# Both gates of a two-layer encoder from seven quarter products: the first gate changed over, and the last weight casts of a gate requeued

## The chip, the cores and the metric

The kernel runs on one core of one Trainium2 chip. The metric is the device time of one execution in microseconds; the time before is the median of three runs. Engines are named as in the profile: PE multiplies matrices (PEld is its weight load), DVE, ACT and POOL work on vectors, SP and others issue transfers.

## The reference

Two layers over 512 tokens of width 1024. Each layer is a mixer (neighbourhood attention, then latent attention) with a SiLU gate and a residual, followed by a gated embedding:

```
for i in range(DEPTH):
    xn = rmsnorm(x, norm_g[i])
    y = mixer_na(...) if i % 2 == 0 else mixer_mla(...)
    h = x + y
    gate = jax.nn.sigmoid(rmsnorm(h, ple_norm[i]) @ ple_w_gate[i])
    x = h + gate * (p[i] @ ple_w_proj[i])
return rmsnorm(x, final_norm)
```

The line with `gate` is what the change is about: a product of 512x1024 by 1024x1024 in each layer.

## The kernel before, in words

All products are made of float32 values split into a high part (`hi`, a rounded copy) and the rest (`lo`): one product of two split operands is three products on PE (hi by hi, lo by hi, hi by lo). So a weight of 128x1024 values costs a load into `wraw`, a copy on ACT (`whi`, L83 or L588) and a subtraction on POOL, sometimes on DVE (`wlo`, L84 or L590), before PE can use it.

The order in time: the embedding products of layer 0 and the first projections; neighbourhood attention in eight pairs of heads (`na_heads`, loop over `j`, each step projecting pair j+1 and attending pair j); the output projection of layer 0 (`out_proj`), the first gate, the latent projection of layer 1 (`mla_c`), latent attention (`mla_heads`), the output projection and gate of layer 1, and the last norm. A framework places the instructions of each engine in a fixed order when the program is built, by a simulated timeline; `issue_after(x)` says that an instruction may not be placed ahead of x. Each engine runs its queue in order.

There are two ways to make a gate. `gate_phase` (used in layer 0 before) takes each of four row tiles of 128 tokens by each of two column halves: 24 products of 512 columns for each of these eight pieces, 192 in all. `gate_seven` (used in layer 1) cuts rows, inner dimension and columns in two and makes the result from seven products of quarters in place of eight, each a quarter of rows in two blocks `i` of 128 tokens by 512 columns: 7 x 2 x 12 = 168 products. It needs sums and differences of the operand's quarters (`keep_half`, `operand`, `mixed`, into tiles X1 to X7) and four sums of the weight's quarters. These are made in DRAM: `sums_begin` issues four copies of 1 MB each on SP's queue, `sums_add` four accumulating transfers on POOL's queue (L528), in three steps, during the first pairs of `na_heads`.

`gate_seven` runs the products in the order 1, 7, 2, 6, 5, 3, 4. `prep(p)` loads, casts and subtracts the two weight pieces of product p. Products 1, 7 and 6 begin a bank of PSUM for each block; 2 adds into 1's, 5 and 3 into 6's, 4 into 7's. Between them ACT copies a bank (`s1`, `s17`, `s6`, the last at L651) and DVE subtracts. `finish(t, n, ...)` makes of a finished bank the sigmoid, multiplies the embedding product to it, adds it to the residual row tile `t`, half `n`, and puts the follow-up (`after`) on a list `behind` that the next `finish` empties. Blocks of product 2 finish half 0 of tiles 0 and 1, of 5 half 1 of tiles 2 and 3, of 3 half 1 of tiles 0 and 1, of 4 half 0 of tiles 2 and 3.

The follow-up in layer 0 is `done`: when both halves of a row tile are there, the tile goes to DRAM (`spill`), its norm is taken (square on ACT, mean on DVE, power on POOL, scaling on DVE), eight transposes on PE turn it and ACT and DVE split it into `x1T`, the operand of `mla_c`. `mla_c` makes first 384 columns for the four row tiles, 24 products each, then 288.

PSUM banks are taken by name: "mm" has 2, "S" 2, "T" 3, "O" 1; transposes use "T".

Of the kernel before, what the change touches and what calls it, by code (L numbers as in the profile page):

```python
# [25 lines left out]
EPS = 1e-6  # L26
# [2 lines left out]
NWARM = 11  # L29
NLATE = 3  # L30
NEARLY = 7
SEVEN = (1,)


def win(t, r0, r1, off, dims):
# [5 lines left out]
class Trunk:  # L41
# [182 lines left out]
    def na_heads(self, pool, xT, zs, oT):  # L224
        nc, a = self.nc, self.a
# [87 lines left out]
        last = project(0)  # L313
        for j in range(8):
            if j < 7:
                last = project(j + 1)
            attend(j)
            for l in SEVEN:
                if j == 0:
                    with self.tc.issue_after(self.last_bias.ins):  # L320
                        self.sums_begin(l)
                elif j < 4:
                    with self.tc.issue_after(self.last_norm.ins):
                        self.sums_add(l, j - 1)
        late = range(8 - NLATE, 8)
        zs.update(self.z_phase(a["na_z"], xT, late, self.last_exp.ins))
        for j in late:
# [242 lines left out]
    def gate_seven(self, pool, layer, rh, res, after):  # L570

        nc = self.nc
        pieces = 0
        turns = 3 + self.wxn // 2
        W, A, Bk, s1, s17, s6 = {}, {}, {}, {}, {}, {}

        def prep(p):
            nonlocal pieces
            W[p] = []
            src = self.quarter[layer][p] if p < 4 else self.sums[layer][p]  # L580
            for c in range(2):
                own = pieces % turns < 3
                pieces += 1
                raw = self.wp.tile([P, 1024], F32, name="wraw", tag="wraw", bufs=3)
                q, n = (self.wp, 3) if own else (pool, self.wxn)
                hi, lo = (q.tile([P, 1024], F32R, name=t, tag=t if own else "w4", bufs=n) for t in ("whi", "wlo"))
                nc.sync.dma_start(raw, src[c * P:(c + 1) * P])
                nc.scalar.activation(hi, raw, AF.Copy)  # L588
                for o in (slice(0, S), slice(S, 2 * S)):
                    nc.gpsimd.tensor_tensor(out=lo[:, o], in0=raw[:, o], in1=hi[:, o].bitcast(F32), op=ALU.subtract)  # L590
                W[p].append((hi, lo))

        behind, loaded = [], self.last_load

        def finish(t, n, ps, o=0, wd=S, last=False):
            x = ps
            sg = nc.scalar.activation(x, x, AF.Sigmoid, scale=rh[t])
# [7 lines left out]
            nc.vector.tensor_tensor(out=x, in0=pe, in1=ps, op=ALU.mult)  # L605
            r = res[t][:, n * S + o:n * S + o + wd]
            (nc.vector if last else nc.gpsimd).tensor_tensor(out=r, in0=r, in1=x, op=ALU.add)
            behind.append(lambda: after(t, n, o, wd))

        mm = self.last_out  # L610
        order = (1, 7, 2, 6, 5, 3, 4)
# [2 lines left out]
        warm = self.small.tile([P, 1], F32, name="warm", tag="ss")  # L614
        nc.scalar.activation(warm, rh[3], AF.Sigmoid)
        halves = ((0, 256), (256, 256)) if layer == 1 else ((0, S),)
        banks = {1: "mm", 7: "T", 6: "S"}
        home = {2: 1, 5: 6, 3: 6, 4: 7}
        C = {}
        sub = lambda out, x, y: nc.vector.tensor_tensor(out=out, in0=x, in1=y, op=ALU.subtract)  # L620
        for k, p in enumerate(order):
            if 0 < k < 4:
                prep(order[k + 3])
            if p == 7:
                self.mixed(5)
# [3 lines left out]
            for i in range(2):  # L629
                for o, wd in halves if i and p in (7, 4) else ((0, S),):  # L630
                    c = slice(o, o + wd)
                    if p in banks:
                        C[p, i, o] = self.psum("O" if o else banks[p])[:, :wd]
                    ps = C[home.get(p, p), i, o]
# [6 lines left out]
                    if p == 1:  # L641
                        s1[i] = self.temp("s1")
                        nc.scalar.activation(s1[i], ps, AF.Copy)
                    elif p == 7:
                        nc.vector.tensor_tensor(out=ps, in0=ps, in1=s1[i][:, c], op=ALU.add)
                        if o == 0:
                            s17[i] = self.temp("s17")
                        nc.scalar.activation(s17[i][:, c], ps, AF.Copy)
                    elif p == 6:
                        s6[i] = self.temp("s6")  # L650
                        nc.scalar.activation(s6[i], ps, AF.Copy)  # L651
                        for (a, b, o), t in C.items():
                            if (a, b) == (7, i):
                                sub(t, t, s6[i][:, o:o + t.shape[1]])
                    elif p == 5:
                        q = self.psum("mm" if i else "T")
                        sub(q, ps, s17[i])
                        sub(ps, ps, s1[i])
                        finish(2 + i, 1, q)
                    elif p == 2:  # L660
                        finish(i, 0, ps, last=True)
                    elif p == 3:
                        finish(i, 1, ps, last=layer == 1)
                    else:
                        finish(2 + i, 0, ps, o, wd, layer == 1)
        while behind:
            behind.pop(0)()

    def mla_c(self, pool, xT, cT, sets):
# [4 lines left out]
        gkv = self.bcast(pool, a["kv_norm"], 256, "gkv")  # L674
        cs = [pool.tile([P, 672], F32, name=f"c{t}", tag="c", bufs=4) for t in range(NT)]
        xh, xl = xT
        toks = (2, 3, 0, 1) if 0 in SEVEN else range(NT)
        L = lambda s, k, t: s[k // 4][:, k % 4, t * P:(t + 1) * P]
        for part, (w0, wn) in enumerate(((0, 384), (384, 288))):
            ws = [self.load_w(a["mla_c"][part][c], 2 * wn, extra=c == 3) for c in range(4)]  # L680
# [263 lines left out]
    def run(self):  # L944
# [4 lines left out]
        def colsT(xT, t):  # L949
            return lambda g: (xT[0][g][:, :, t * P:(t + 1) * P], xT[1][g][:, :, t * P:(t + 1) * P])  # L950
# [57 lines left out]
        x1T = []  # L1008
        for layer in range(2):
            with tc.tile_pool(name=f"out{layer}", bufs=4, reuse_waits="tile") as pool:  # L1010
# [8 lines left out]
                if layer == 0:  # L1019
                    gn = self.bcast(pool, a["norm_g"][1], D, "gn")  # L1020
                hnT, rh = {}, {}
                if seven:
                    self.row_scale(layer)
# [24 lines left out]
                if layer == 1:  # L1048
                    with self.tc.issue_after(self.last_load.ins):
                        gn = self.bcast(pool, a["final_norm"], D, "gn")  # L1050
                seen = set()
                if layer == 0:
                    def done(t, n, o, w):
                        if t not in seen:
                            seen.add(t)
                            return
                        nc.sync.dma_start(self.spill[t], res[t])
                        xn = pool.tile([P, D], F32, name="x1n", tag="xn", bufs=2)
                        self.rms(xn, res[t], gn, D, self.rows[1][0][:, t:t + 1])
                        if not x1T:  # L1060
                            x1T.extend([[self.bigtile(f"x1{s}{g}") for g in range(2)] for s in "hl"])
                        self.rows_to_cols(xn, colsT(x1T, t))
                else:
                    mean = {}

# [142 lines left out]
```

## Time and profile before

| | us |
|---|---|
| median of 3 runs (lowest to highest) | 664.75 (663.46 to 665.41) |
| the profiled execution | 664.26 |
| its span, first to last instruction | 662.5 |
| PE busy | 652.7 (99%) |
| ACT busy | 423.6 (64%) |
| POOL busy | 411.1 (62%) |
| DVE busy | 382.5 (58%) |
| products of the first gate on PE, first to last start | 282.0 to 328.1 |
| products of the second gate on PE, first to last start | 614.3 to 654.0 |

The profile is of one execution. Busy time of PE counts matrix products that overlap one another, so its pace is read from the starts of products in a row (the chain that ended last gives pieces with their length and count) and not from their durations. A group's row gives line, engine, operation, output and inputs, shapes and count, then its busy time, the mean of one in ns, and the idle time of the engine ahead of it with what ended it. A row of the waits gives the engine and line that waited, what for, the sum in us, how often, and the longest.

### The profile page before, as it was taken

The page shows a single profiled execution, that of the slowest core. Times are in us where ns is not written, and L with a number is a line of the kernel's source. Part 1 is how long each engine was busy: PE and PEld are TensorE (multiplying, and loading weights), DVE is VectorE, ACT ScalarE, POOL GpSimd, SP SyncE. Part 2 cuts the span into 40 slices and gives each one's busy share as a digit, 9 for nine tenths or more (in the row PEclk, how much of TensorE's full clock was granted, in tenths as well). Part 3 has the DMA queues.
Part 4 walks back from the last instruction along what each step waited for, and adds up shares of the span by engine and source line. Part 5 has one row for each costly group of instructions (what it writes and reads, how often), then busy time and mean ns, then how long its engine had stood idle before and what let it go on. Part 6 is the DMA issues. An engine that isn't in the chain of part 4 may idle for free.

```text
span 662.5 us, 10039 instructions
## 1 busy us (share of the span) xinstructions
PE 652.7 (99%) x3443; PEld 555.6 (84%) x3443; DVE 382.5 (58%) x821; ACT 423.6 (64%) x840; POOL 411.1 (62%) x350
## 2 busy tenths in 40 slices
PE   9999999999999999999999999999999999999995
PEld 6888888988988888888899888888888888888874
DVE  6280565746546414453623623888888876464955
ACT  7671686857767742653444545888979897537845
POOL 0395465785575665853154625695959878436973
PEclk9999999999999999999999999999999999999998
DMA  9949422976242128443133334220211213573424
GB/s 325 345 149 339 152 88 89 195 160 153 74 138 90 64 89 307 160 135 130 74 116 105 106 104 144 72 76 0 62 59 63 65 65 128 213 295 128 170 84 159
DMA packets 37682, 90.63 MB, mean 137 GB/s; under 512 B 4416, under 2 KB 13376, under 8 KB 37568
## 3 DMA queue, kind: packets, MB, share of 16 engines
q1 hardware_dynamic: 33040, 85.02, 37.2%
q0 software_dynamic: 4160, 4.19, 4.1%
q10 hardware_dynamic: 432, 0.79, 0.3%
q8 instruction: 27, 0.44, 0.3%
q14 instruction: 23, 0.19, 0.1%
HBM read 78.45 MB, written 16.78 MB: 144 GB/s over the span
## 4 chain that ended last, share of the span: by engine, by line
PE 96%; POOL 1%; ACT 1%; issue 1%; DVE 1%; DMA 0%; POOLq 0%
PE ps_mm L107 42%; PE ps_S L107 13%; PE ps_mm L734 6%; PE ps_T L139 6%; PE ps_O L845 4%; PE ps_T L107 3%; PE ps_O L107 3%; PE ps_S L639 3%; PE ps_T L238 2%; PE ps_O L402 2%; PE ps_mm L639 2%; PE ps_mm L184 2%; PE ps_T L390 2%; PE ps_S L354 1%; PE ps_S L353 1%; PE ps_O L238 1%
## 5 line engine op out<-in xcount | busy, mean ns | idle before, releaser
L84 POOL TENSOR_TENSOR wwlo<-wraw,wwhi 128x1024 fp32r<-128x1024 f32 (+5 forms) x92 | 175.9, 1928 | 107.1 <-ACT wwhi L83 92.7
L83 ACT ACTIVATE wwhi<-wraw 128x1024 fp32r<-128x1024 f32 (+5 forms) x94 | 79.1, 863 | 74.8 <-issue 18.9
L830 POOL TENSOR_TENSOR ex<-ex,rc 128x512 f32<-128x512 f32 x64 | 66.3, 1047 | 24.8 <-DVE rc L829 18.1
L828 ACT ACTIVATE ex<-ps_S,mx 128x512 f32<-128x512 f32 x64 | 44.0, 688 | 11.8 <-DVE mx L826 10.7
L96 DVE TENSOR_TENSOR pt_lo<-ps_T,pt_hi 128x512 fp32r<-128x512 f32 x64 | 43.3, 682 | 7.7 <-ACT pt_hi L94 7.3
L826 DVE TENSOR_REDUCE mx<-ps_S 128x1 f32<-128x512 f32 x64 | 43.7, 682 | 6.8 <-PE ps_S L107 6.2
L376 POOL TENSOR_TENSOR ex<-ex,rc 128x128 f32<-128x128 f32 (+1 forms) x64 | 34.8, 584 | 18.2 <-DVE rc L372 18.2
L590 POOL TENSOR_TENSOR wlo<-wraw,whi 128x512 fp32r<-128x512 f32 x28 | 36.7, 1348 | 7.8 <-ACT whi L588 7.7
L107 PE MATMUL ps_mm<-xh,wwhi 128*128 128x512 f32 x152 | 40.9, 399 | 0.2 <-DVE sb L270 0.2
L94 ACT ACTIVATE pt_hi<-ps_T 128x512 fp32r<-128x512 f32 x64 | 37.7, 595 | 4.2 <-PE ps_T L139 3.9
L139 PE MATMUL ps_T<-ident,ex 128*128 128x128 f32 x256 | 38.4, 272 | 0.0
L107 PE MATMUL ps_mm<-xl,wwhi 128*128 128x512 f32 x152 | 38.2, 390 | 0.0
L107 PE MATMUL ps_mm<-xh,wwlo 128*128 128x512 f32 x152 | 38.0, 390 | 0.0
L139 PEld LDWEIGHTS ps_T<-ident,ex 128*128 128x128 f32 x256 | 31.5, 140 | 7.7 <-POOL ex L830 0.4
L107 PE MATMUL ps_mm<-wwhi,hnT 128*128 128x512 f32 x128 | 35.0, 392 | 0.0
L107 PEld LDWEIGHTS ps_mm<-xl,wwhi 128*128 128x128 f32 x152 | 28.4, 188 | 5.8
L107 PEld LDWEIGHTS ps_mm<-xh,wwlo 128*128 128x128 f32 x152 | 28.3, 188 | 5.8
L205 DVE TENSOR_TENSOR u<-ps_O,u 64x512 f32<-64x512 f32 x32 | 21.9, 686 | 18.2 <-ACT u L204 17.7
L107 PEld LDWEIGHTS ps_mm<-xh,wwhi 128*128 128x128 f32 x152 | 27.3, 188 | 5.3 <-ACT wwhi L83 0.6
L370 ACT ACTIVATE ex<-ex,mx 128x128 f32<-128x128 f32 (+1 forms) x64 | 30.3, 475 | 1.8 <-DVE mx L360 0.8
L107 PE MATMUL ps_S<-ke,qe 96*128 96x512 f32 x96 | 29.0, 408 | 0.0
L107 PE MATMUL ps_S<-ko,qo 128*128 128x512 f32 x96 | 28.9, 409 | 0.0
(437 smaller groups left out, 1775.1 us busy)
## 6 DMA issues: line engine op xcount, KB each, us to landing
wraw<-na_qk SPq DMA_DIRECT2D x16, 512.0 KB, 3.4
pe<-pe SPq DMA_DIRECT2D x31, 256.0 KB, 5.4
wraw<-gate SPq DMA_DIRECT2D x14, 512.0 KB, 3.3
wraw<-na_v SPq DMA_DIRECT2D x8, 512.0 KB, 3.9
wraw<-na_o SPq DMA_DIRECT2D x8, 512.0 KB, 3.2
wraw<-mla_z SPq DMA_DIRECT2D x8, 512.0 KB, 3.5
wraw<-mla_o SPq DMA_DIRECT2D x8, 512.0 KB, 3.6
wraw<-sum SPq DMA_DIRECT2D x8, 512.0 KB, 3.2
```

The costliest lines, as they stand in the source:

```text
L83: nc.scalar.activation(hi[:, c], raw[:, c], AF.Copy)
L84: f = lambda e, c=c: e.tensor_tensor(out=lo[:, c], in0=raw[:, c], in1=hi[:, c].bitcast(F32), op=ALU.subtract)
L94: self.last_copy = nc.scalar.activation(hi, src, AF.Copy, scale=scale)
L96: nc.vector.tensor_tensor(out=lo, in0=src, in1=hi.bitcast(F32), op=ALU.subtract)
L107: last = self.last_mm = nc.tensor.matmul(out, l, r, start=i == 0, stop=i == n - 1)
L139: self.last_mm = self.nc.tensor.transpose(t[:, i * P:(i + 1) * P], b, self.ident)
L376: self.last_norm = nc.gpsimd.tensor_tensor(out=e, in0=e, in1=rc[:, qt:qt + 1].to_broadcast([P, e.shape[1]]), op=ALU.mult)
L590: nc.gpsimd.tensor_tensor(out=lo[:, o], in0=raw[:, o], in1=hi[:, o].bitcast(F32), op=ALU.subtract)
L734: self.last_mm = nc.tensor.matmul(PS[key], *terms[i], start=i == 0, stop=i == len(terms) - 1)
L826: nc.vector.reduce_max(mx, sp, axis=AX.X, negate=True)
L828: nc.scalar.activation(ex, sp, AF.Exp, bias=mx, accum_out=sm)
L830: nc.gpsimd.tensor_tensor(out=ex, in0=ex, in1=rc.to_broadcast([P, S]), op=ALU.mult)
```

## The change

Layer 0's gate is made by `gate_seven` too. Its weight sums are begun and added in pairs 0 to 3 of `na_heads`, those of layer 1 now in pairs 4 to 7. The weight pool of layer 0's stage takes the size that layer 1's has (`wxn` 10), by which `out_proj` also makes every other low part on DVE.

In `gate_seven`, for both layers: the last product's weights (4) are prepared when the second block of product 6 is copied, with their casts queued behind that copy, and not a product earlier; products 7 and 6 swap banks "T" and "S". For layer 0: products 5, 3 and 4 add their result on DVE and product 2's on POOL, and the follow-up of the former is issued at once and not put on the list. `done` of layer 0 takes the square and the mean of each half as it comes, and scales, turns and splits half by half. The norm weights of layer 1 (`gn`) are loaded after the last weight load of `out_proj`.

```diff
-SEVEN = (1,)
+SEVEN = (0, 1)
...
-            for l in SEVEN:
-                if j == 0:
-                    with self.tc.issue_after(self.last_bias.ins):
-                        self.sums_begin(l)
-                elif j < 4:
-                    with self.tc.issue_after(self.last_norm.ins):
-                        self.sums_add(l, j - 1)
+            l, step = divmod(j, 4)
+            if step == 0:
+                with self.tc.issue_after(self.last_bias.ins):
+                    self.sums_begin(l)
+            else:
+                with self.tc.issue_after(self.last_norm.ins):
+                    self.sums_add(l, step - 1)
...
-        def prep(p):
+        def prep(p, after=None):
...
-                nc.scalar.activation(hi, raw, AF.Copy)
+                with self.tc.issue_after(after.ins) if after else nullcontext():
+                    nc.scalar.activation(hi, raw, AF.Copy)
...
-            behind.append(lambda: after(t, n, o, wd))
+            if layer == 0 and last:
+                after(t, n, o, wd)
+            else:
+                behind.append(lambda: after(t, n, o, wd))
...
-        banks = {1: "mm", 7: "T", 6: "S"}
+        banks = {1: "mm", 7: "S", 6: "T"}
...
-            if 0 < k < 4:
+            if k in (1, 2):
                 prep(order[k + 3])
...
-                        nc.scalar.activation(s6[i], ps, AF.Copy)
+                        copy = nc.scalar.activation(s6[i], ps, AF.Copy)
+                        if i:
+                            prep(order[-1], copy)
...
-                        finish(2 + i, 1, q)
+                        finish(2 + i, 1, q, last=layer == 0)
                     elif p == 2:
-                        finish(i, 0, ps, last=True)
+                        finish(i, 0, ps, last=layer == 1)
                     elif p == 3:
-                        finish(i, 1, ps, last=layer == 1)
+                        finish(i, 1, ps, last=True)
                     else:
-                        finish(2 + i, 0, ps, o, wd, layer == 1)
+                        finish(2 + i, 0, ps, o, wd, True)
...
-        toks = (2, 3, 0, 1) if 0 in SEVEN else range(NT)
+        toks = range(NT)
...
                 if layer == 0:
+                    mean = {}
+
                     def done(t, n, o, w):
-                        if t not in seen:
-                            seen.add(t)
+                        r = res[t]
+                        sq = pool.tile([P, S], F32, name="sq", tag="hg", bufs=3)
...
+                        nc.scalar.activation(sq, r[:, n * S:(n + 1) * S], AF.Square, accum_out=ss)
+                        nc.vector.tensor_scalar(mn, ss, 1.0 / D, mean.get(t, EPS), op0=ALU.mult, op1=ALU.add)
+                        if t not in mean:
+                            mean[t] = mn
                             return
-                        nc.sync.dma_start(self.spill[t], res[t])
-                        xn = pool.tile([P, D], F32, name="x1n", tag="xn", bufs=2)
-                        self.rms(xn, res[t], gn, D, self.rows[1][0][:, t:t + 1])
+                        rs = self.small.tile([P, 1], F32, name="rs", tag="rs")
+                        nc.gpsimd.tensor_tensor(out=rs, in0=mn, in1=self.half, op=ALU.pow)
+                        nc.gpsimd.tensor_scalar(self.rows[1][0][:, t:t + 1], mn, 1.0, None, op0=ALU.add)
+                        nc.sync.dma_start(self.spill[t], r)
...
-                        self.rows_to_cols(xn, colsT(x1T, t))
+                        xn = pool.tile([P, D], F32, name="x1n", tag="xn", bufs=2)
+                        for g in range(2):
+                            c = slice(g * S, (g + 1) * S)
+                            nc.vector.scalar_tensor_tensor(xn[:, c], r[:, c], rs, gn[:, c], op0=ALU.mult, op1=ALU.mult)
+                            b = self.transposes([xn[:, (4 * g + i) * P:(4 * g + i + 1) * P] for i in range(4)])
+                            hi, lo = colsT(x1T, t)(g)
+                            self.split(hi, lo, b.rearrange("p (a b) -> p a b", a=4))
```

More of the change, by code (lines that the diff above doesn't have):

```diff
@@ L1018, in run @@
                 gp = self.bcast(pool, a["ple_norm"][layer], D, "gp")
-                if layer == 0:
-                    gn = self.bcast(pool, a["norm_g"][1], D, "gn")
                 hnT, rh = {}, {}
@@ L1047, in run @@
                 self.out_proj(a["na_o"] if layer == 0 else a["mla_o"], oT, res, turn_h, last)
-                if layer == 1:
-                    with self.tc.issue_after(self.last_load.ins):
-                        gn = self.bcast(pool, a["final_norm"], D, "gn")
+                with self.tc.issue_after(self.last_load.ins):
+                    gn = self.bcast(pool, a["final_norm"] if layer else a["norm_g"][1], D, "gn")
                 seen = set()
                 if layer == 0:
+                    mean = {}
@@ L1053, in done @@
                     def done(t, n, o, w):
-                        if t not in seen:
-                            seen.add(t)
+                        r = res[t]
+                        sq = pool.tile([P, S], F32, name="sq", tag="hg", bufs=3)
+                        ss = self.small.tile([P, 1], F32, name="ss", tag="ss")
+                        mn = self.small.tile([P, 1], F32, name="mn", tag="mn")
+                        nc.scalar.activation(sq, r[:, n * S:(n + 1) * S], AF.Square, accum_out=ss)
```

## The prediction

> **What bounds the kernel now.** I read the page first (span, engine shares, the chain that ended last), then the waits of PE, then the pieces of the chain in order of time, then the groups by shape and the busy time of each engine by stage.
>
> ```profile
> span 662.5 us, 10039 instructions
> ...
> PE 652.7 (99%) x3443; PEld 555.6 (84%) x3443; DVE 382.5 (58%) x821; ACT 423.6 (64%) x840; POOL 411.1 (62%) x350
> ...
> PE 96%; POOL 1%; ACT 1%; issue 1%; DVE 1%; DMA 0%; POOLq 0%
> ```
>
> PE carries 96% of the chain. A busy PE need not be a PE at its pace, so the second question is whether it ever waits. The whole list of waits of PE:
>
> ```profile
> PE ps_T L956 <- PEq L1197: 0.8, 1, 0.8
> PE ps_S L639 <- ACT s L651: 0.7, 1, 0.7
> PE ps_mm L107 <- DVE sb L270: 0.2, 1, 0.2
> ```
>
> Inside the work PE waits 0.9 us in all. The chain's pieces (start, length, what, how many) give the pace at which products come:
>
> ```profile
> 320.83 0.87 PE ps_T L139 x8
> ...
> 332.55 3.13 PE ps_mm L107 x18
> ...
> 614.44 5.45 PE ps_mm L639 x24
> ...
> 631.41 5.45 PE ps_S L639 x24
> 637.54 11.21 PE ps_S L639 x48
> ```
>
> A product of 512 columns costs 5.45 / 24 = 0.227 us, one of 384 columns (the latent projection that follows the first gate) 3.13 / 18 = 0.174 us, a transpose 0.87 / 8 = 0.109 us. The piece that begins at 631.41 ends at 636.86 and the next begins at 637.54: that 0.68 us is the wait on L651 above. So the kernel is a queue of products: what leaves that queue is gained, if nothing that feeds it becomes late. The Trainium skill, "TensorE: Matmul & The Clock Gate", section "Back-to-back issue gap", gives 131 ns sustained and N/2.4 + 2.5 = 216 ns isolated for 512 columns; by these the 24 products of the next part would be 3.1 or 5.2 us, and the trace, with 0.227 us, agrees with neither, so its own pace is used.
>
> **Part 1: the products of the first gate.** The first gate's stage, groups by shape:
>
> ```profile
> L107 PE MATMUL ps_mm<-wwhi,hnT 128*128 128x512 f32 x128 | 35.0, 392 | 0.0
> L107 PE MATMUL ps_mm<-wwlo,hnT 128*128 128x512 f32 x64 | 19.9, 391 | 0.0
> ```
>
> These 192 products of 512 columns become 7 quarter products x 2 blocks x 12 = 168, all still of 512 columns (the split into 256 is for layer 1 only). The transposes stay 4 per half row tile. So 24 x 0.227 = 5.45 us leave PE, which has no slack: **-5.45 us**, if its feeders keep up. The next three parts ask whether they do.
>
> **Part 2: the wait on L651 in the second gate.**
>
> ```profile
> 635.95 1.06 ACT L588 ACTIVATE whi<-wraw 128x1024 fp32r<-128x1024 f32 x1 [2.69 <-DMA wraw<-sum]
> 636.91 1.07 ACT L651 ACTIVATE s<-ps_S 128x512 f32<-128x512 f32 x2
> ```
>
> ACT stood 2.69 us for a weight of the last product and then cast it, while both copies of product 6 (the fourth in order) waited behind it on ACT; product 5 adds into the banks that they read and so waited too. The change queues both casts of the last product behind the second copy. Gone: **-0.68 us**. What is late next is that weight itself: two casts of 1.06 us and four subtractions on POOL (next row, 1.35 us each, 5.4 us) start some 0.6 us after product 6 and end about 7 us after it; products 5 and 3 take 48 x 0.227 = 10.9 us meanwhile, so 3 to 4 us of cover are left. Without that cover each microsecond is paid in full. The loads keep their place on SP's queue, they only hold two raw buffers longer.
>
> **Part 3: weights and sums.**
>
> ```profile
> L590 POOL TENSOR_TENSOR wlo<-wraw,whi 128x512 fp32r<-128x512 f32 x28 | 36.7, 1348 | 7.8 <-ACT whi L588 7.7
> ```
>
> ```profile
> L84 POOL TENSOR_TENSOR wwlo<-wraw,wwhi 128x1024 fp32r<-128x1024 f32 x13 | 31.0, 2411 | 8.7 <-ACT wwhi L83 5.2 <-PE ps_T L139 3.5
> ```
>
> ```profile
> 183.00:236.00 53.00, 53.00 (x292) 45.70 (x291) 25.99 (x88) 35.67 (x81) 35.49 (x36) 1.00 0.27 91
> 291.00:328.50 37.50, 37.50 (x175) 31.23 (x174) 16.77 (x23) 13.94 (x21) 8.40 (x10) 1.00 0.33 116
> 614.30:654.10 39.80, 39.11 (x197) 33.01 (x195) 28.76 (x48) 26.77 (x49) 32.56 (x27) 1.00 0.37 131
> ```
>
> (The columns of the last fence: stretch, length, then busy time of PE, PEld, DVE, ACT, POOL, granted clock, DMA share, GB/s.) (The two POOL rows are groups of the stretches 591 to 654 and 246 to 290.) Today POOL makes the low parts of 8 + 8 weights of projection and gate in layer 0: 16 x 2.41 = 38.6 us. After, half of the projection's go to DVE (the larger weight pool switches that on), so POOL has 4 x 2.41 + 28 x 1.35 = 47.4 us, 8.8 more. In the first gate's stretch (291 to 328.5) POOL is busy 8.40 of 37.5 us, so 29 us stand open; and the second gate (614 to 654) already runs this same list with POOL at 32.56 of 39.8 us and PE at 39.11. I take 0; the bounds are 0 and the 8.8 us if POOL had no gap.
>
> The sums of the first gate are four copies inside DRAM on SP's queue at head pair 0 and four accumulating transfers on POOL's queue at pairs 1 to 3; those of the second gate move to pairs 4 to 7. Their price on POOL:
>
> ```profile
> L528 POOL DMA_DIRECT2D sum<-gate x2: 1519/1666/1812, 117.7 to 118.8; - x2
> L528 POOL DMA_DIRECT2D sum<-sum x2: 1272/1286/1300, 130.7 to 157.2; - x2
> ```
>
> The added set is 2 x 1.67 + 2 x 1.29 = 5.9 us of POOL, in a part where it is busy 35.49 of 53 us (183 to 236) while PE never stops. Queued behind each is the scaling of the probabilities for the next transposes, and on SP the loads behind the copies. Bounds 0 and 5.9 us; near 0, since the same four in the earlier pairs stand in no wait of PE. I take **+0.2 us**. The broadcast of the norm weights moves behind the last projection load and is first read tens of microseconds later: nothing. Products 7 and 6 swap banks: nothing in layer 1.
>
> **Part 4: the handover from the first gate to the latent projection.** Today the eight (row, half) pieces end 5.45 us apart, with a whole one spare between row tiles. After, the blocks of 12 products (2.72 us) end in the order 5, 5, 3, 3, 4, 4, and the last four each complete a row tile: tile 0 is complete 36 x 0.227 = 8.2 us before the gate's end, tile 1 5.4, tile 2 2.7, tile 3 at the end. The next stage wants them 0, 4.2, 8.4 and 12.5 us after it (24 x 0.174 = 4.2 each). So each has 8.2, 9.6, 11.1 and 12.5 us. Durations of the steps, from the second gate, where the same steps run, and from today's handover:
>
> ```profile
> 648.77 0.66 ACT L597 ACTIVATE ps_S<-ps_S,rs 128x512 f32<-128x512 f32 x1 [1.19 <-PE ps_S L639]
> 649.36 0.62 ACT L1077 ACTIVATE sq<-r 128x512 f32<-128x512 f32 x1
> 649.88 0.19 ACT L1077 ACTIVATION_READ_ACCUMULATOR sq<-r 128x1 f32 x1
> ```
>
> ```profile
> 649.47 0.70 DVE L605 TENSOR_TENSOR ps_S<-pe,ps_S 128x512 f32<-128x512 f32 x1 [1.24 <-ACT ps_S L597]
> 650.10 0.21 DVE L1078 TENSOR_SCALAR mn<-ss,mn 128x1 f32<-128x1 f32 x1
> 650.23 0.68 DVE L607 TENSOR_TENSOR r<-r,ps_S 128x512 f32<-128x512 f32 x1
> 650.98 0.75 DVE L1088 SCALAR_TENSOR_TENSOR r<-r,rs,gn 128x512 f32<-128x512 f32 x1
> ```
>
> ```profile
> 314.32 0.56 POOL L123 TENSOR_TENSOR rs<-ss,half 128x1 f32<-128x1 f32 x1
> ```
>
> ```profile
> L94 ACT ACTIVATE x1h<-ps_T 128x512 fp32r<-128x512 f32 x8 | 4.4, 596 | 8.7 <-PE ps_T L139 8.7
> ```
>
> ```profile
> L96 DVE TENSOR_TENSOR x1l<-ps_T,x1h 128x512 fp32r<-128x512 f32 x8 | 5.2, 685 | 4.8 <-ACT x1h L94 4.8
> ```
>
> Sigmoid 0.66, multiply 0.70, add 0.68, square 0.62 + 0.19, mean 0.21, power 0.56, scaling 0.75, four transposes 0.44, copy 0.60, rest 0.68: 6.1 us to the first half of a tile's columns; the second half (0.75 + 0.68 more) is wanted 12 x 0.174 = 2.1 us later. Tile 0 has 8.2 us. But tile 1's multiply and add (1.4 us) fall in front of its scaling on DVE, and its power on POOL can meet a weight's subtraction (1.35 us, on average half): 6.1 + 1.4 + 0.7 = 8.2, with nothing over for ten hand-overs between engines. I take **+1.0 us** late at PE for these; bounds 0 and the price of the DVE rival below.
>
> **Sum.** -5.45 - 0.68 + 0.2 + 1.0 = -4.9 us. The profiled execution took 664.26 us (span 662.5 and 1.8 around it), so 659.3; it lay 0.5 us under the median of the three runs (664.75), on which basis the forecast is 659.8 us. About 0.3%, 2 us here, is what a measurement can tell.
>
> **Rivals.** *Slower: DVE sets the handover.* From the first block of product 5 (13.6 us before the gate's end) to the moment tile 3 is wanted (12.5 after) are 26.1 us. DVE has in them per tile 0.70 + 0.68 + 0.21 + 2 x 0.75 + 2 x 0.685 = 4.46, four times 17.8, and for product 5 twice two subtractions (0.70 each), multiply, add and mean, 6.0: 23.8 us, 2.3 spare. The scalings read two operands from SBUF, and such a one has this spread:
>
> ```profile
> L1030 DVE SCALAR_TENSOR_TENSOR hg<-r,rowb,gp x8: 740/752/2553, 585.5 to 616.9; 128x512 f32<-128x512 f32 x8
> ```
>
> If all eight took 2.55 us, DVE would have 14.4 us more, tile 3 would be 12.1 late, and the kernel stands at 664.75 - 5.9 + 12.1 = 671. The point from which it decides: 2.3 + 5.9 = 8.2 us, an average of 1.8 us for the eight. For it: POOL will be subtracting the next stage's weights just then. Against it: the median is 0.752, and 2.55 stands at the end of eight. The Trainium skill, "GPSIMD Engine Reference", section "Specifications", says POOL shares SBUF interfaces with VectorE and contends with its instructions of two SBUF inputs; by that rule the long ones would be the usual case here and this rival the outcome, and the trace, with one long row against a median of 0.752, bears it out only in part.
>
> *Half the gain.* PE takes its queue in order, and the transposes of four tiles stand between products at places fixed when the program is built. If two of the tiles' transposes are each 1 to 2 us late there, 2 to 4 us go: 662 to 664.
>
> *The feeders of the first gate.* If POOL starts the 28 subtractions late (it needs 37.7 us of the 38.2 us that PE will take), the 8.8 us of part 3 show in part, say 3 to 8: 662 to 667. Against it: the second gate.
>
> *Not what it says:* 24 products leave by count; only the 0.68 us of part 2 could stay, the copy being late for another reason: 660.5, inside the forecast.
>
> **How the numbers follow.** Forecast 0.60 (658.4 to 661.3: both small terms at 0, up to 2.5 us of lateness); half the gain 0.18; feeders 0.08; DVE 0.14 (666 to 671). Faster by over 0.3% (under 662.75): all of the first, half of the second, a quarter of the third: 0.71. Slower (over 666.75): the DVE case and a little of the feeders: 0.15. Within: 0.14. The range leaves out the DVE case and the late part of the feeders above and a few in a hundred below: 657.8 to 665.0.
>
> **What would show it.** Right: 168 products on L639's line in a stretch near 282 to 322, no wait of PE on the copy of product 6, waits of PE between 315 and 335 of 1 us or so in all, on x1 operands from DVE or ACT. Wrong: a wait of several microseconds there with DVE busy throughout and scalings of 2 us; a wait on low weights from POOL between 282 and 320; or new PE waits on scaled probabilities between 120 and 236.

## The result, and the profile after

The changed kernel is slower: 666.78 us (median of 15 runs, 665.60 to 667.62) against 664.41 us of the kernel before (15 runs, 663.28 to 665.67), a ratio of 1.0034 with a 95% interval of 1.0025 to 1.0043. Forecast were 659.8 us (range 657.8 to 665.0) and "faster". The profiled execution took 667.25 us.

The page of the changed kernel, span, PE's row and the shares of the chain that ended last:

```profile
span 665.4 us, 10116 instructions
...
PE 651.3 (98%) x3419; PEld 552.2 (83%) x3419; DVE 401.5 (60%) x854; ACT 438.7 (66%) x875; POOL 429.8 (65%) x375
...
PE 89%; DVE 3%; POOL 3%; ACT 2%; issue 2%; DMA 1%; POOLq 0%; ACTq 0%
```

The 24 products are gone (3443 to 3419), and yet the span grew by 2.9 us. The chain says why: 96% of it lay on PE before, 89% now. Something feeds PE late. Its waits (engine, line, what for, the sum in us, how often, the longest):

```profile
PE ps_T L643 <- ACT s L655: 1.8, 1, 1.8
PE ps_O L402 <- ACT ph L94: 1.2, 1, 1.2
PE ps_T L962 <- PEq L1215: 0.8, 1, 0.8
PE ps_S L353 <- ACT da L285: 0.6, 1, 0.6
PE ps_mm L107 <- ACT x1h L94: 0.4, 1, 0.4
PE ps_mm L467 <- ACT whi L446: 0.3, 1, 0.3
```

The wait of the second gate is gone. At the start of the kernel 0.8 us is as before, and 0.3 (L467) is added. Three places inside the work are new: the neighbourhood attention (L402 and L353, 1.2 and 0.6), the first gate (L643, 1.8), and the handover, that is the passage from the first gate to the latent projection (L107, 0.4). The waits in these three places make 4.0 us, not the 7.9 us by which the span missed its forecast (665.4 against 662.5 - 4.9). So I set the places of the same products in the two traces side by side (starts of products, us):

| stretch | before | after | change | forecast |
|---|---|---|---|---|
| span's start to the last product of the first output projection | 280.94 | 284.47 | +3.5 | +0.2 |
| from there to the first score product of the second attention (gate 1, handover, latent projection) | 130.57 | 130.27 | -0.3 | -5.45 + 1.0 |
| from there to the first product of gate 2 | 202.76 | 202.95 | +0.2 | 0 |
| gate 2, first to last product | 39.77 | 38.76 | -1.0 | -0.68 |
| from there to the span's end | 8.41 | 9.00 | +0.6 | 0 |

Two lines carry the miss: the first (3.3 us) and the second (4.2 us).

**The first line: a value weight that lands late.** Between 138 and 158 us the neighbourhood attention loads its next value weights. The view of the tile of raw weights gives the time from issue to landing of the loads in this stretch, first of the kernel before, then of the changed one:

```profile
DMA to landing us min/median/max: 3.2/4.1/4.3
```

```profile
DMA to landing us min/median/max: 9.9/13.9/14.8
```

The windows of the same 10 us, before and after (columns as in the prediction's windows; the last three are granted clock, DMA share, GB/s):

```profile
140.00:150.00 10.00, 10.00 (x46) 8.27 (x45) 3.11 (x5) 4.03 (x6) 7.37 (x5) 1.00 0.41 125
```

```profile
140.00:150.00 10.00, 10.00 (x45) 8.21 (x44) 3.04 (x5) 2.77 (x4) 7.06 (x4) 1.00 1.02 328
```

The queues of SP and POOL show what fills the DMA engines: the four copies of the second gate's sums, now at pair 4, and just ahead of them an accumulation of the first gate's, which is under way all through them: it lands 29.2 us after its issue at 129.15, where the one at 130.74 in the kernel before took 12.5 us.

```profile
133.39 2.40 SPq L522 DMA_DIRECT2D sum<-gate  x4
139.84 2.69 SPq L82 DMA_DIRECT2D wraw<-na_v  x2
```

```profile
129.15 1.30 POOL L528 DMA_DIRECT2D sum<-sum  x1 [0.74 <-DMA sum<-gate]
```

And ACT's timeline shows who pays. Before, then after (start, length, what; the idle time before it):

```profile
148.75 1.06 ACT L83 ACTIVATE wwhi<-wraw 128x1024 fp32r<-128x1024 f32 x1 [2.48 <-issue]
150.53 0.59 ACT L284 ACTIVATE da<-ps_mm 64x512 fp32r<-64x512 f32 x1 [0.71 <-PE ps_mm L107]
```

```profile
154.69 1.06 ACT L83 ACTIVATE wwhi<-wraw 128x1024 fp32r<-128x1024 f32 x1 [8.72 <-PE ps_mm L107]
155.78 0.59 ACT L284 ACTIVATE da<-ps_mm 64x512 fp32r<-64x512 f32 x1
...
158.21 0.49 ACT L94 ACTIVATE ph<-ps_T 128x384 fp32r<-128x384 f32 x1
```

ACT stands idle for 8.72 us ahead of one cast. The row names PE's product as the last to release it, but the load decides: the first of the two value loads was issued at 139.84 and landed 14.8 us later, at 154.6, and the cast starts at 154.69. In the kernel before the same cast started at 148.75, with its load landed at 144.4. Behind the cast, on an engine that takes its queue in order, stand the copies `da` and `ph`, which PE's scores and transposed probabilities need at once. PE does not wait for the weight; it waits for what is queued behind the weight's cast.

**The second line: product 2's additions.** The chain that ended last, between 305 and 321 us (start, length, what):

```profile
305.46 2.54 POOL wlo L591 x2
307.99 1.70 POOL r L608
309.74 0.51 issue
310.25 0.19 ACT sq L1063
310.44 0.49 ACT s L655
310.97 10.08 PE ps_T L643 x36
```

Read upwards: PE's product 5 waits for the copies of product 6 (L655) on ACT; these stand behind a square of the finished half row (L1063); the square waits for the addition of product 2 to the residual (L608), which layer 0 does on POOL; and that starts when the low parts of weights (L591) are done. The place behind the low parts costs little: the multiply that feeds the addition ends on DVE at 307.72, 0.2 us before the addition starts. What costs is the addition itself, 1.70 us here. The piece at the end has 36 products in 10.08 us, 0.28 us each and not 0.227. The windows say why (the clock is the third number from the end):

```profile
309.00:310.00 1.00, 0.15 (x1) 0.00 (x0) 0.14 (x1) 0.28 (x1) 1.00 (x2) 1.00 0.80 212
...
312.00:313.00 1.00, 1.00 (x4) 0.80 (x3) 0.25 (x1) 1.00 (x2) 0.51 (x1) 0.50 0.75 225
...
314.00:315.00 1.00, 1.00 (x4) 0.72 (x3) 0.00 (x0) 0.00 (x0) 1.00 (x2) 0.51 0.00 0
```

PE stood for 1.8 us, took up work again at 311, and was then granted half its clock until 315 (1.00 again in the slice after), a product of 512 columns every 0.43 us. Below, "lost" means this: the distance of the starts of two products, less the pace of their shape, summed over a stretch. By that count the first gate loses 4.4 us between 300 and 317, the attention 3.9 between 150 and 170, and the handover 1.4.

### The profile page after: what moved, and what is told of

The parts are those of the page before. It is cut to its first block, busy times and chain, and to the rows that moved or that the text cites. A ratio compares the mean times of both kernels' runs of the same rounds, so it can differ in the third digit from the quotient of the medians.

```text
span 665.4 us, 10116 instructions
## 1 busy us (share of the span) xinstructions
PE 651.3 (98%) x3419; PEld 552.2 (83%) x3419; DVE 401.5 (60%) x854; ACT 438.7 (66%) x875; POOL 429.8 (65%) x375
## 4 chain that ended last, share of the span: by engine, by line
PE 89%; DVE 3%; POOL 3%; ACT 2%; issue 2%; DMA 1%; POOLq 0%; ACTq 0%
PE ps_mm L107 35%; PE ps_S L107 13%; PE ps_mm L740 6%; PE ps_T L139 5%; PE ps_O L851 4%; PE ps_T L643 4%; PE ps_T L107 3%; PE ps_O L107 3%; PE ps_T L238 2%; PE ps_O L402 2%; PE ps_mm L643 2%; PE ps_mm L184 2%; PE ps_T L390 2%; PE ps_S L354 1%; PE ps_S L353 1%
## 5 line engine op out<-in xcount | busy, mean ns | idle before, releaser
L84 POOL TENSOR_TENSOR wwlo<-wraw,wwhi 128x1024 fp32r<-128x1024 f32 (+5 forms) x78 | 143.7, 1855 | 84.3 <-ACT wwhi L83 71.6
L83 ACT ACTIVATE wwhi<-wraw 128x1024 fp32r<-128x1024 f32 (+5 forms) x81 | 65.5, 832 | 62.8 <-PE ps_mm L107 23.7
L591 POOL TENSOR_TENSOR wlo<-wraw,whi 128x512 fp32r<-128x512 f32 x56 | 73.9, 1350 | 22.7 <-ACT whi L589 19.5
L107 PE MATMUL ps_mm<-xh,wwhi 128*128 128x512 f32 x152 | 40.2, 397 | 0.0
L107 PE MATMUL ps_mm<-xl,wwhi 128*128 128x512 f32 x152 | 38.5, 391 | 0.0
L107 PE MATMUL ps_mm<-xh,wwlo 128*128 128x512 f32 x152 | 38.1, 391 | 0.0
L107 PEld LDWEIGHTS ps_mm<-xh,wwlo 128*128 128x128 f32 x152 | 28.4, 188 | 6.0
L107 PEld LDWEIGHTS ps_mm<-xl,wwhi 128*128 128x128 f32 x152 | 28.3, 188 | 5.7
L589 ACT ACTIVATE whi<-wraw 128x1024 fp32r<-128x1024 f32 x28 | 29.2, 1055 | 5.0 <-DMA wraw<-sum 2.6
L209 POOL TENSOR_TENSOR u<-u,z 128x512 f32<-128x512 f32 x16 | 21.3, 1334 | 16.5 <-DVE u L205 8.7
L107 PEld LDWEIGHTS ps_mm<-xh,wwhi 128*128 128x128 f32 x152 | 27.3, 188 | 4.9
L643 PE MATMUL ps_T<-whi,X 128*128 128x512 f32 x96 | 27.4, 408 | 2.0 <-ACT s L655 1.8
```

Source lines behind the costliest of these rows:

```text
L83: nc.scalar.activation(hi[:, c], raw[:, c], AF.Copy)
L84: f = lambda e, c=c: e.tensor_tensor(out=lo[:, c], in0=raw[:, c], in1=hi[:, c].bitcast(F32), op=ALU.subtract)
L107: last = self.last_mm = nc.tensor.matmul(out, l, r, start=i == 0, stop=i == n - 1)
L643: mm = nc.tensor.matmul(ps, l, r, start=j == 0 and p in banks, stop=j == 11 and p in (2, 3, 4), skip_group_check=True)
```

## The experiments

Two theories for the attention: the copies alone, moved to pair 4, hold up the loads; or the copies together with the first gate's accumulations do. Two for the gate: product 2's additions on POOL, or DVE's queue (the prediction's slow case). And one question: is the low clock a cause of lost time, or only a mark of it?

**e1: product 2's additions on DVE, in the changed kernel.**

```diff
...
-                        finish(i, 0, ps, last=layer == 1)
+                        finish(i, 0, ps, last=True, now=False)
```

(`now=False` keeps its square and mean on the list `behind`, as they were.)

> The changed kernel with one edit: in layer 0 product 2's two additions to the residual run on DVE and not on POOL; their follow-up stays on the list, and the placed order of ACT and PE is the same. Theory A (a POOL addition behind weight subtractions keeps a square waiting on ACT, the copies of product 6 wait behind the square, PE waits 1.83 us for them, and then runs some 3.5 us at a lower granted clock, 4.4 us in all between 305 and 316): the wait of PE on the copy is gone, clock 1.00 in 311 to 317, time 4.0 to 4.4 us under the changed kernel's 666.8, about 662.5. Rival (the clock falls there for another reason, such as the load on PE itself): 1.8 us less at most, 665. Rival (the DVE queue is the bound of this stretch, as the slow case of the prediction had it): no gain, or slower, since DVE gets two more operations of 0.69 us.

664.93 us (664.30 to 665.97), 1.0010 of before [1.0000, 1.0020]: 1.9 us better than the change by the medians, 2.5 by the spans (665.4 to 662.9), and less than was expected. The wait on the copy in its list of waits:

```profile
PE ps_T L643 <- ACT s L655: 0.6, 1, 0.6
```

1.8 became 0.6, the clock stays at 1.00 in the gate, and the gate loses 1.4 us in place of 4.4. The square ahead of the copies, in the changed kernel and in e1:

```profile
309.71 0.63 ACT L1063 ACTIVATE sq<-r 128x512 f32<-128x512 f32 x1 [1.38 <-POOL r L608]
```

```profile
308.52 0.63 ACT L1063 ACTIVATE sq<-r 128x512 f32<-128x512 f32 x1
```

It starts 1.2 us earlier, because the addition takes 0.69 us on DVE (from 307.80) and not 1.70 on POOL (from 307.94). So in the changed kernel the additions on POOL are the larger part of the gate's loss; 0.6 us of the wait have another cause (e8).

**e2: the second gate's four copies issued one each at pairs 1 to 4, in the changed kernel.**

```diff
...
+            if 1 <= j <= 4:
+                with self.tc.issue_after(self.last_bias.ins):
+                    self.sums_begin(1, (j - 1,))
...
```

> The changed kernel with one edit: the four copies in DRAM for the second gate's sums are issued one each at head pairs 1, 2, 3 and 4 and not all four at pair 4. Theory B (8 MB of traffic in one burst makes a value weight land 12 us late, its cast stands first on ACT's queue for 8.7 us, key copies and exponentials wait behind it and PE with them, 3.9 us with the clock that falls after it): those 3.9 us shrink to under 0.5, time 3.3 to 3.9 us under 666.8, about 663. Rival (the accumulating transfers on POOL, not the copies, cost the time): no change over 0.5 us, since they stay where they are.

662.24 us (661.91 to 665.34), 0.9978 [0.9969, 0.9988]: 4.5 us better than the change. The attention loses 0.0 us between 150 and 170; the gate's wait of 1.8 us is still there. (The profiled execution, 665.34 us, has a wait of 1.2 us near 77 us on DVE that no other trace shows.)

**e3: both edits.**

> The changed kernel with both edits: product 2's additions on DVE, and the copies for the second gate one each at pairs 1 to 4. If theories A and B hold and are independent, both gains add up: 666.8 - 4.2 - 3.6 = 659 us, 5.4 us under the kernel before (the prediction's 659.8 nearly), with 1 us of waits left at the handover to the latent projection. If the handover takes over what is freed (the slow case of the prediction), 662 or more.

660.73 us (660.20 to 660.97), 0.9949 [0.9936, 0.9961]. It is 6.05 us better than the change; the two edits alone gave 1.85 + 4.54 = 6.4. The two causes are separate and add up.

**e4: the kernel before, with nothing changed but the place of the second gate's copies and accumulations (pairs 4 to 7).**

```diff
-                if j == 0:
+                if j == 4:
...
-                elif j < 4:
+                elif j > 4:
...
-                        self.sums_add(l, j - 1)
+                        self.sums_add(l, j - 5)
```

> The kernel before with one part of the change alone: the second gate's copies and accumulating transfers move from head pairs 0 to 3 to pairs 4 to 7; the first gate stays as it was, with 192 products. Theory B: 3 to 4 us slower than the kernel before, 667.5 to 668.5, with the same wait of ACT for a value weight near 145 to 155. Rival (it is the doubled number of transfers, or their accumulations, that hurts): no change, 664.4, since the count of transfers is that of the kernel before.

664.22 us, 1.0002 [0.9994, 1.0011]: no cost. The landing of the loads between 138 and 158 us, and the cast on ACT:

```profile
DMA to landing us min/median/max: 3.3/7.9/11.4
```

```profile
151.24 1.06 ACT L83 ACTIVATE wwhi<-wraw 128x1024 fp32r<-128x1024 f32 x1 [5.41 <-DMA wraw<-na_v]
```

The copies do delay the value weight, by 7 us (4.3 to 11.4), and its cast by 2.5 (148.75 to 151.24). The kernel before has that to spare: PE does not wait. The first theory falls: the copies alone cost nothing that the interval shows.

**e5: the kernel before, with nothing but the last product's casts queued behind product 6's second copy.**

```diff
...
-            if 0 < k < 4:
+            if k in (1, 2):
...
+                        if i:
+                            prep(order[-1], copy)
```

> The kernel before with the second part of the change alone: the last product's weights are prepared at the second copy of product 6, their casts queued behind it (banks as before, first gate as before, 192 products). The prediction's step: the 0.68 us wait of PE on the copy goes and 0.7 us is gained, 663.4 against 664.1. Rival (the work behind the last product, its weight and the end of the row tiles, gives it back): no difference, the last product ends earlier and the span does not.

663.22 us, 0.9992 [0.9983, 1.0000]; the span is 661.4, and of the waits only the start's 0.8 us is left. The gain is 1.1 us by the spans, 0.9 by the medians and 0.5 by the ratio, whose interval just reaches 1: in the trace the wait is gone, in the times the gain is at the edge of what can be told.

**e6: eight products of a constant, 512 columns each, ahead of product 5 of the first gate in the changed kernel.** They write a bank that is not used, and keep PE busy where it stood for 1.8 us.

```diff
...
+                    if layer == 0 and p == 5 and i == 0:
+                        idle = self.psum("O")
+                        for _ in range(8):
+                            with self.tc.issue_after(mm.ins):
+                                mm = nc.tensor.matmul(idle, *ones, start=True, stop=True)
```

> The changed kernel with eight products of constants (128x512, bfloat16, into a bank that nothing reads, about 1.7 us) placed on PE ahead of product 5 of the first gate, where PE waits 1.8 us for the copy. Theory C (about half of the 4.4 us lost there is a lower granted clock that follows an idle PE): the wait on the copy stays as late as it was, PE is busy through it, the granted clock in the 6 us after it is 1.00 and not 0.76, and the time falls by 2 to 2.5 us, 664.5. Rival (the slow products after the wait are slow for their own operands or banks): the time stays at 666.8 or rises.

667.95 us (666.52 to 669.44), 1.0054 [1.0040, 1.0067]: slower by 1.2 than the change, not faster. But the gate did what the clock theory says. PE's timeline, the changed kernel and then e6 (its trace holds seven of the eight products):

```profile
310.97 1.60 PE L643 MATMUL ps_T<-whi,X 128*128 128x512 f32 x4 [1.83 <-ACT s L655]
313.23 1.89 PE L643 MATMUL ps_T<-whi,X 128*128 128x512 f32 x4
```

```profile
309.44 1.69 PE L644 MATMUL ps_O<-const-bfloat16-1.0 128*128 128x512 bf16 x7
311.19 1.21 PE L649 MATMUL ps_T<-whi,X 128*128 128x512 f32 x4
```

Product 5 began as late as before (311.19, 310.97), but at full pace: from there to the gate's last product 16.3 us passed (311.19 to 327.45) against 17.8 (310.97 to 328.81). So the half clock alone costs 1.6 us. What was won came back as loss at the handover, where PE stood twice, 1.21 and 0.69 us, and the clock fell there:

```profile
331.00:332.00 1.00, 0.34 (x1) 0.34 (x2) 1.00 (x2) 0.99 (x2) 0.76 (x2) 0.90 0.00 0
332.00:333.00 1.00, 1.00 (x5) 0.87 (x5) 1.00 (x3) 0.34 (x2) 0.00 (x0) 0.50 0.67 266
```

The loss at the handover is 4.1 us in place of 1.4. DVE is busy 0.96 to 1.00 of each slice from 328 to 335. In e6 four additions and multiplies stand between its first and its second pair of scalings, in the changed kernel one, and the second pair starts at 329.38 and not 328.14: the eight products shifted the order in which the program is laid out. The time of e6 is thus no test of the clock; its gate is.

**e7: the first gate's second and third accumulations at pairs 5 and 6, away from the second gate's copies, in the changed kernel.**

```diff
-            else:
+            for l, step in {1: [(0, 1)], 5: [(1, 1), (0, 2)], 6: [(1, 2), (0, 3)], 7: [(1, 3)]}.get(j, ()):
```

> The changed kernel with one edit: the second and third accumulating transfers of the first gate's sums come after pairs 5 and 6 and not 2 and 3, so that none is under way when the second gate's four copies are issued at pair 4; copies and count are as in the changed kernel. The moved sums alone cost the kernel before nothing measurable (664.2 against 664.0), their value weight being cast at 151.2 against 154.7 in the changed kernel. Theory B2 (copies plus the accumulation that runs beside them make it late; either alone fits into the slack of 2.5 us): cast at 151 to 152, wait under 0.5 us, time 3 to 3.5 us under 666.8. Rival B1 (the copies at pair 4 are enough in the changed kernel): no change.

662.58 us (660.93 to 667.17), 0.9974 [0.9958, 0.9990]: 4.2 us better than the change. The loads:

```profile
DMA to landing us min/median/max: 3.1/7.7/11.2
```

That is e4's delay (11.4), not the change's (14.8), with the same copies at pair 4; the attention loses nothing at 150 to 170. So it is copies and accumulation together. The trace also shows what an accumulation costs on POOL when it is not ready. POOL's timeline:

```profile
219.72 1.27 POOL L528 DMA_DIRECT2D sum<-sum  x1
225.27 1.27 POOL L528 DMA_DIRECT2D sum<-sum  x1 [4.28 <-DMA sum<-sum]
226.05 2.62 POOL L376 TENSOR_TENSOR ex<-ex,rc 128x128 f32<-128x128 f32 x4
```

The second waits 4.28 us for the first to land, the scaling of probabilities queues behind it, and PE loses 4.4 us between 224 and 232, again with the clock at 0.50 after it (229 to 231). The first gate, on the other hand, loses nothing: from the projection's last product to the first score product it is 125.9 us, 4.7 less than before. So the 4.2 us are a sum of three: 3.9 won in the attention, 4.4 won in the gate, 4.4 lost at 224 to 232.

Product 2's additions are still on POOL in e7. POOL's timeline, the changed kernel and then e7:

```profile
307.94 2.96 POOL L608 TENSOR_TENSOR r<-r,pe 128x512 f32<-128x512 f32 x2
```

```profile
305.46 2.66 POOL L608 TENSOR_TENSOR r<-r,pe 128x512 f32<-128x512 f32 x2
```

They come 2.5 us earlier. ACT's queue is laid out in another order in e7, and product 2's two sigmoids start at 303.15 and 304.20, not at 306.18 and 307.70. So the additions on POOL need not cost PE time: it depends on when ACT's order lets them start.

**e8: e3, with the operands of product 3 issued behind the second copy of product 6, and product 2's squares behind that.**

```diff
-            while behind and (o or wd == S):
+            while behind and (o or wd == S) and (layer or p != 2):
...
-            if p == 6:
-                self.mixed(3)
...
+                            with self.tc.issue_after(copy.ins):
+                                self.mixed(3)
```

> The version with both edits (product 2's additions on DVE, copies spread over pairs 1 to 4; 660.7) with ACT's queue cleared ahead of product 6's copies: the operand of product 3 is made behind the second copy, and the squares of product 2's halves come after it. If the 0.6 us wait of PE and the slow products around it (1.4 us over the pace in 300 to 310) come from ACT's queue order there: 0.8 to 1.4 us less, 659.6. If DVE, busy 4.6 to 5.0 of each 5 us from 295 to 305, sets it: no gain.

660.52 us (660.14 to 660.61), 0.9940 [0.9929, 0.9952]: the lowest median here, 0.6% under the kernel before, but only 0.2 us under e3, which the intervals do not tell apart. The wait on the copy is gone and the gate loses 0.0 us (e3: 1.5). It comes back behind it: the handover loses 2.0 us in place of 1.4, and the stretch from the last product to the end is 10.0 us and not 9.2. The longest wait in the list is now

```profile
PE ps_mm L107 <- ACT x1h L94: 1.1, 2, 0.7
```

**e9: e8, with product 4's additions of the first gate on POOL.**

```diff
...
-                        finish(2 + i, 0, ps, o, wd, True)
+                        finish(2 + i, 0, ps, o, wd, True, own=layer == 0)
```

> The kernel of e8 (660.5 us; 2.0 us of PE time lost between 320 and 330, at the handover to the latent projection) with one thing changed in the first gate alone: the multiply of product 4 writes to the loaded sum instead of its bank, and its addition to the residual (two row tiles, 512 columns each) is done on POOL (about 1.3 us each, POOL is under 1 us busy in 320 to 325) instead of DVE (0.69 us each, DVE is busy 4.92 of 5 us in 320 to 325). If DVE sets the handover (the rival of the prediction): the scaling of row tile 1 and the low parts come up to 1.4 us earlier, the loss falls from 2.0 to about 1.0, and the run gives about 659.7. If the handover is set by the places that the transposes and the high-part copies have in PE's and ACT's order behind the gate's last product, the loss stays near 2 us and the time at 660.5. If the later sums (0.6 us more each on POOL) reach the transposes of the last two row tiles, the loss grows and the time is above 661.

661.53 us (661.19 to 663.07), 0.9956 [0.9940, 0.9973]: the third outcome. The median is 1.0 us over e8's, though the intervals of the two overlap; in the trace the handover loses 3.0 us and not 2.0. DVE's and POOL's timeline:

```profile
319.18 1.41 DVE L1082 SCALAR_TENSOR_TENSOR x1n<-r,rs,gn 128x512 f32<-128x512 f32 x2
...
323.09 2.45 DVE L1082 SCALAR_TENSOR_TENSOR x1n<-r,rs,gn 128x512 f32<-128x512 f32 x2
```

```profile
323.21 1.78 POOL L613 TENSOR_TENSOR r<-r,pe 128x512 f32<-128x512 f32 x1
```

The relief that DVE got in additions it paid back at once: beside POOL's addition two scalings take 2.45 us in place of 1.41, and that addition 1.78, where the one before it on POOL took 1.26. The Trainium skill, "GPSIMD Engine Reference", section "Specifications", says that POOL shares its SBUF interfaces with VectorE (DVE here) and contends with VectorE's instructions of two SBUF inputs; these rows agree. The run also moved transposes behind products, so it doesn't say what DVE's additions alone cost at the handover.

## Why the prediction was wrong

Two steps failed, in two places: the price of the sums in part 3, and the condition of part 1.

- *Part 3, the sums, +0.2.* This step failed, by 3.3 us (3.5 measured). It looked for the price on POOL (5.9 us of issue) and read "no wait of PE" in the earlier pairs as proof that the copies are free. The price was in the DMA engines: a value weight landed 14.8 us after its issue instead of 4.3, and ACT's queue carried that on to PE. "On SP the loads behind the copies" was written down, but no price was worked out. e4 shows that the step would have been right for the move alone, and e2, e3 and e7 that the move beside the first gate's accumulations is what costs. The sign to look for, "new PE waits on scaled probabilities between 120 and 236", was nearly right in place, but the waits are on ACT's copies. In e7, where two accumulations met, the wait on scaled probabilities came too (2.1 and 0.5 us).
- *Part 1, -5.45, "if its feeders keep up".* The count (24) and the pace hold: with the stalls out, gate, handover and latent projection together take 4.7 us less in e7, where the prediction had 5.45 - 1.0 = 4.45. The condition failed in the changed kernel: the gate loses 4.4 us. Product 2's two additions on POOL, and what stands ahead of product 6's copies in ACT's queue, had no row in the sum. With the additions on DVE 3.0 of the 4.4 go (e1): 1.2 of them are wait, 1.6 the low clock that followed it (e6). The other 1.4 go with ACT's order ahead of the copies (e8), and in e7 another order of ACT lets the additions stay on POOL at no cost. The sign "no wait of PE on the copy of product 6" held in the second gate and failed in the first (1.8 us).
- *Part 3, the low weights, 0.* Near: no PE wait names a low weight, and product 2's first addition stands behind one for only 0.2 us. The rival of the feeders had the right engine, POOL, and the wrong reason. Its 662 to 667 us (chance 0.08) hold the result partly by luck, as 3.3 us of the miss came from the attention, which it does not name.
- *Part 2, -0.68.* Right, and a little small: -1.0 in the stretch of products, in the changed kernel and alone (e5), and the weight that was made late is nowhere waited for.
- *Part 4, +1.0.* Right: the handover loses 1.4 us in the changed kernel, and the same count gives the kernel before 0.4 in that stretch, so 1.0 is added. In e8 the loss is 2.0. DVE's timeline and PE's, in the changed kernel:

```profile
325.92 1.41 DVE L1077 SCALAR_TENSOR_TENSOR x1n<-r,rs,gn 128x512 f32<-128x512 f32 x2
```

```profile
329.04 1.47 PE L139 MATMUL ps_T<-ident,x1n 128*128 128x128 f32 x12
331.44 0.62 PE L107 MATMUL ps_mm<-wwhi,x1h 128*128 128x384 f32 x2 [0.35 <-ACT x1h L94]
```

  Tile 0 is scaled at 327.3, 1.7 us ahead of the gate's last product, but its transposes stand behind that product in PE's queue, with 12 in a row.
- *The DVE rival, 0.14.* Its mechanism did not come: all eight scalings of the changed kernel took 744 to 755 ns. But e6 and e9 show that DVE is full there, and that a later scaling is paid for.
- *What stays open:* the 0.6 us at the end of the changed kernel. Its last instructions are e5's, 4.8 us from the last product to the last issue in both; the last transfer then ends 0.5 us later. And why accumulation and copies together delay a load by 3 us more than the copies alone was not measured by itself; the rows show only that the accumulation beside them is slow too (29.2 us to landing, 12.5 in the kernel before).

## What to carry to other kernels

A transfer that no engine waits for still has a price where it shares the DMA engines with a load that is just in time: price it by the time from issue to landing of the loads behind it, and then ask what is queued behind the consumer of that load on its engine. When an operation is moved to an engine because it has time to spare, look at how long it takes there, what stands ahead of it in the queues and who waits at the end of the chain, not at the engine's busy share. And stalls add up in their own places but are not given back one for one: of the 1.5 us that e8 won in the gate, 0.6 was lost again in the handover behind it. When one edit changes the order in which the whole program is laid out, read the place that was edited in the trace, and not the total.

## What the runs showed of the hardware

- After PE had stood for 1.8 us, its granted clock was 0.50 for 3.4 us (311.56 to 314.97 in the trace's clock record), and products of 512 columns came every 0.43 us; the cost was 1.6 us on top of the wait. The same fall, 3.41 us long each time, came after 1.8 us in e2, after 2.1 us in e7 and after 1.21 and 0.69 us close together in e6. It did not follow the wait of 1.2 us in e2. The two waits in the attention (0.6 and 1.2 us in the changed kernel, 0.7 and 1.2 in e1) were followed by no fall in the changed kernel, but by 0.50 from 158.8 to 162.2 in e1, where it cost little (4.1 us lost there, 3.9 in the changed kernel).
- The clock records let these cases be told apart. In each trace the falls and rises lie whole multiples of 3.413 us apart. On that grid PE stood 1.8 to 2.1 us in the step right ahead of each fall, and at most 1.2 us in every other step between the clock's first rise and a kernel's last product. The attention's two waits lay in one step in e1 (1.8 us together) and in two in the changed kernel (1.0 and 0.8). So by these runs the limit lies somewhere between 1.2 and 1.8 us of standing in one step. The Trainium skill, "TensorE: Matmul & The Clock Gate", Part 1, has half clock after an idle window of about 3.4 us, counted by a window that runs freely; the half, the length of the slow stretch and the free-running grid agree with these rows, but a stand of half that length was enough.
- Four copies inside DRAM (the second gate's sums) hold up a load on the same queue by 7 us (4.3 us to landing in the kernel before, 11.4 in e4), and by 10.5 us with an accumulation beside them (14.8).
